# Routing in two parts, and combine's identity products ordered behind the last expert

## The chip, the cores and the metric

The kernel runs on one core of one Trainium2 chip. The number that counts is the device time of one execution in microseconds (us). The core has five engines that run side by side, each through its own instructions strictly in order: TensorE (PE in the profile, with its weight loads as PEld), VectorE (DVE), ScalarE (ACT), GpSimd (POOL) and SyncE (SP), which here only issues loads. An instruction whose operands are not ready holds back everything that stands behind it on its engine.

## The reference

The model is two layers (DEPTH 2) on 512 tokens of width 1024. A layer is a token mixer with three branches and then a mixture of experts. Only the second half matters here:

```python
def grouped_moe(x, router_w, router_b, w1, w3, w2):       # x: 512 tokens x 1024
    logits = (xt @ router_w).astype(jnp.float32) + router_b
    scores = jax.nn.softmax(logits, axis=-1)               # 16 experts in 4 groups of 4
    grp_score = lax.top_k(scores.reshape(T, 4, 4), 2)[0].sum(-1)
    best = jnp.argmax(grp_score, axis=-1)                  # one group for each token
    in_group = (jnp.arange(16) // 4)[None, :] == best[:, None]
    top_w, top_e = lax.top_k(jnp.where(in_group, scores, -1.0), 2)
    gates = top_w / jnp.sum(top_w, axis=-1, keepdims=True)
    ...                                                    # tokens sorted by expert
    hb = jax.nn.silu(xb @ w1[e]) * (xb @ w3[e])
    return hb @ w2[e]                                      # 1024 x 1024 weights each
    ...                                                    # gated rows summed back per token

h = layer_norm(ALPHA * h + y, ln2_g[l], ln2_b[l])
```

So each token goes to the two best experts of its best group, and its output is the gated sum of two expert rows plus the residual, normalised.

## The kernel before

**Arithmetic.** Nearly all products are in 32-bit floating point made of three reduced products: a weight tile `raw` of 128x1024 is split into a rounded part `wh` (a cast on ScalarE, L342) and the rest `wl` (a subtraction on VectorE, L343), activations likewise, and `mm3` (L345 to L350) adds high x high, high x low and low x high. Lines 348, 349 and 350 are thus nearly all of TensorE's work. A split into `wl` that names GpSimd as its engine runs there: this is done for the first four tiles of the first expert of each layer.

**Tokens** come in four blocks of 128 (NT is 4), and everything that depends on a token is laid out as 128 partitions by 4 blocks.

**Routing.** After the mixer, `logits` makes the 128x16 logits of one block at a time: transposes, products with the router weights into the PSUM bank `lg` (a bank of kind "o", of which there is one), and two VectorE instructions (L1057, L1058) that apply the norm to them. `keep_awake` then puts 15 dummy products on TensorE (L1081). `route` (L1083 on) works on all four blocks at once: the row maximum `mx`, the difference `s`, the exponential on ScalarE, some 19 small VectorE instructions that end in the 0/1 matrix `M` (L1118) of each token's two experts, then eight small products that count, for each token, how many earlier tokens chose the same expert (L1122, L1125) and how many chose each expert in all (L1128). They go to a bank `rk`. The rank within the expert is `rke` (L1131); `cn` (L1133) is a copy of the counts.

**Gather products.** `one_hot` (L1244) compares `rke` with an iota and gives a 0/1 matrix `A`, one 128x256 piece per block, for the first two experts. 64 products (L1358: 4 blocks by 8 column chunks k by 2 for the high and low half of the token rows) pick the tokens of those experts into eight banks `gx`; banks of the chunks 0 to 6 are of other kinds, the last chunk's is the bank "o". The token rows of the last block are normalised just before by `settle`, which is told to come behind the exponential and behind the last piece of `A`: two ScalarE instructions (L296), four on VectorE (L299), two casts to the high half on ScalarE (L1071) and two subtractions for the low half on VectorE (L1072). Then the chunks are copied to `hx` and the experts begin. `gates` (L1141 on) makes the gate weights with small VectorE instructions meanwhile.

**Experts and combine.** Fourteen experts have 96 fixed slots each. Their outputs go to DRAM (`yd`), except those of two experts, of which one is the last: they stay on the chip as `ywh` and `ywl` (`last_y`, L1487 and L1488). At the end of the layer `collect` gathers for each block c the two expert rows of each token with indirect DMAs from GpSimd's queue into `yg` (L1467) and adds the two (L1473): the left half of the columns on VectorE, the right half on GpSimd, both issued behind the last weight split. `add_known` (L1447) starts the sum of a block in two PSUM banks `cmb` with what is known, and `combine` adds the sum `yg` by a product with the identity matrix (L1559) and the last expert's rows by two products (L1561). There are eight identity products in a layer, two for each block. The norm of the result follows; in the last layer it is the end of the program.

**What sets the order.** The program is written for a scheduler that puts the instructions of each engine in one fixed order by priority and expected readiness; `issue_after(x)` forbids it to place an instruction ahead of x, without adding a wait. On TensorE this fixed order is what counts below, since a product early in it that waits for another engine stops all the later ones.

## Time and profile before

| | |
|---|---|
| runs, us | 2222.1, 2217.58, 2212.92 (median 2217.58) |
| profiled execution, us | 2214.86 |
| its span, first to last instruction, us | 2213.1 |
| TensorE busy | 2114.7 us, 96% |
| VectorE busy | 1545.0 us, 70% |
| ScalarE busy | 1230.4 us, 56% |
| GpSimd busy | 505.0 us, 23% |
| mean granted TensorE clock | 0.976 |

The span is the time between the first and the last instruction on the core; the 1.8 us around it belong to the execution but show no instruction. A busy share is a mean over stages, so the table says only that TensorE is the engine that most stages wait for: a microsecond that TensorE loses is mostly a microsecond of the time, and one that another engine loses is felt only where TensorE waits for it or at the very end.

### The profile page before, as it was taken

Reading aid. Unit: us, or ns where it says so; the run is one execution under the profiler, and the core shown is the slowest. Engines: PE = TensorE matmul, PEld = TensorE weight load, DVE = VectorE, ACT = ScalarE, POOL = GpSimd, SP = SyncE. Lnnn points to the kernel's source line nnn. Section 1 sums busy time; section 2 is a strip of 40 time slices with the busy share of each in tenths; the row PEclk is TensorE's granted clock in tenths of the full one; section 3 lists DMA queues with packets and bytes.
Section 4 is the critical chain, followed back from the end, with each engine's and each line's share of the span. In section 5 each row is a group of like instructions: output and inputs, shape, how many; then the busy total and the mean of one; then the engine's idle time right before and its main releaser. Section 6 shows DMA issues by size and latency. Waiting matters only on the chain. (4 is left out here: it accounts for less than half of the span.)

```text
span 2213.1 us, 27508 instructions
## 1 busy us (share of the span) xinstructions
PE 2114.7 (96%) x10178; PEld 1557.3 (70%) x10181; DVE 1545.0 (70%) x1986; ACT 1230.4 (56%) x1548; POOL 505.0 (23%) x535
## 2 busy tenths in 40 slices
PE   6999999998999999998899999999899999999987
PEld 5668678876777766665666877888767776666664
DVE  8443533459999899887663535434799998888877
ACT  4333123336888777776544331223488887777763
POOL 5410142122039825000260202411410000000004
PEclk9988999999999999999999999999999999999999
DMA  5121275337999999998731213352499999999973
GB/s 192 54 52 53 65 246 194 103 121 280 385 346 375 375 368 340 376 379 315 260 138 45 76 57 124 105 190 96 148 347 386 388 385 352 380 364 380 365 301 130
DMA packets 192461, 533.16 MB, mean 241 GB/s; under 512 B 18545, under 2 KB 72433, under 8 KB 192306
## 3 DMA queue, kind: packets, MB, share of 16 engines
q1 hardware_dynamic: 173312, 476.69, 58.2%
q0 software_dynamic: 8032, 28.84, 3.9%
q10 hardware_dynamic: 10962, 25.67, 3.4%
q8 instruction: 84, 1.38, 0.3%
q14 instruction: 71, 0.58, 0.1%
HBM read 501.14 MB, written 27.00 MB: 239 GB/s over the span
## 5 line engine op out<-in xcount | busy, mean ns | idle before, releaser
L343 DVE TENSOR_TENSOR wl<-raw,wh 128x1024 fp32r<-128x1024 f32 x850 | 1042.3, 1261 | 345.5 <-ACT wh L342 310.6
L342 ACT CAST wh<-raw 128x1024 fp32r<-128x1024 f32 x872 | 896.0, 1050 | 426.7 <-PE e L350 152.8
L349 PE MATMUL e<-wl,hx 128*96 128x512 f32 x1024 | 408.9, 399 | 9.4 <-DVE wl L343 9.4
L350 PE MATMUL e<-wh,hx 128*96 128x512 f32 x1024 | 408.2, 399 | 0.0
L348 PE MATMUL e<-wh,hx 128*96 128x512 f32 x1024 | 383.4, 397 | 10.0 <-PEq L1496 9.9
L348 PE MATMUL pjf<-hx,wh 128*128 128x512 f32 x608 | 244.7, 403 | 4.8 <-DVE v L215 4.8
L350 PE MATMUL pjf<-hx,wl 128*128 128x512 f32 x608 | 244.2, 402 | 2.5 <-DVE wl L343 2.5
L349 PE MATMUL pjf<-hx,wh 128*128 128x512 f32 x608 | 244.6, 402 | 0.8 <-DVE hx L216 0.7
L349 PEld LDWEIGHTS e<-wl,hx 128*96 128x96 f32 x1024 | 167.0, 163 | 86.0 <-DVE wl L343 20.0
L348 PEld LDWEIGHTS e<-wh,hx 128*96 128x96 f32 x1024 | 166.4, 163 | 78.9 <-issue 11.4
L350 PEld LDWEIGHTS e<-wh,hx 128*96 128x96 f32 x1024 | 166.9, 163 | 66.1 <-issue 0.6
L349 PE MATMUL e<-wl,gh 128*96 128x512 f32 x512 | 204.0, 398 | 5.9 <-DVE wl L343 5.4
L350 PE MATMUL e<-wh,gl 128*96 128x512 f32 x512 | 201.2, 394 | 2.6 <-DVE gl L1267 2.6
L1182 POOL DMA_INDIRECT xr<-xd,idx x28 | 46.3, 1655 | 655.8 <-PE tx L1264 523.2
L348 PE MATMUL e<-wh,gh 128*96 128x512 f32 x512 | 180.2, 394 | 0.0
L348 PEld LDWEIGHTS pjf<-hx,wh 128*128 128x128 f32 x608 | 115.9, 191 | 33.4 <-DVE v L215 6.0
L350 PEld LDWEIGHTS pjf<-hx,wl 128*128 128x128 f32 x608 | 115.7, 190 | 29.5 <-DVE wl L343 3.0
L349 PEld LDWEIGHTS pjf<-hx,wh 128*128 128x128 f32 x608 | 115.7, 190 | 29.2 <-DVE hx L216 1.9
L349 PEld LDWEIGHTS e<-wl,gh 128*96 128x96 f32 x512 | 82.6, 161 | 49.8 <-DVE wl L343 18.1
L348 PEld LDWEIGHTS e<-wh,gh 128*96 128x96 f32 x512 | 82.5, 161 | 35.3
L350 PEld LDWEIGHTS e<-wh,gl 128*96 128x96 f32 x512 | 82.5, 161 | 35.2 <-DVE gl L1267 3.5
L956 POOL TENSOR_TENSOR mg<-mg,gsg 128x512 f32<-128x512 f32 x32 | 42.9, 1345 | 211.6 <-DVE gsg L955 187.3
(500 smaller groups left out, 2823.4 us busy)
## 6 DMA issues: line engine op xcount, KB each, us to landing
raw<-in_moe_w_dram SPq DMA_DIRECT2D x384, 1024.0 KB, 7.7
raw<-in_w_in_dram SPq DMA_DIRECT2D x44, 1024.0 KB, 5.3
yd<-y ACTq DMA_DIRECT2D x28, 384.0 KB, 6.0
raw<-in_w_out_dram SPq DMA_DIRECT2D x8, 1024.0 KB, 5.0
yd<-zr ACTq DMA_DIRECT2D x14, 384.0 KB, 5.2
row<-hd POOLq DMA_DIRECT2D x8, 512.0 KB, 7.1
rawu<-in_w_up_c_dram SPq DMA_DIRECT2D x8, 512.0 KB, 3.4
xd<-row POOLq DMA_DIRECT2D x8, 512.0 KB, 3.6
```

The source lines that it names most:

```text
L342: self.cut = (nc.scalar.copy(hv, v).ins, (eng or nc.vector).tensor_tensor(lv, v, hv.bitcast(F32), OP.subtract).ins)
L343: (eng or nc.vector).tensor_tensor(lv, v, hv.bitcast(F32), OP.subtract).ins)
L348: mm(out, lh, rh, start=start, stop=False)
L349: mm(out, lh, rl, start=False, stop=False)
L350: mm(out, ll, rh, start=False, stop=stop)
L956: nc.gpsimd.tensor_tensor(mg[m], mg[m], sg, OP.add)
L1182: self.fetched = self.nc.gpsimd.indirect_dma_start(out=t, out_offset=None, in_=self.x_dram[:, :], in_offset=at).ins
```

## The change

1. `route` runs its chain of small instructions twice: for the blocks 0 to 2 together, then for block 3. Ranks of the first part depend on the first three blocks alone, so `A` of these blocks can be made before the last block's logits have gone through the chain. The counts are summed once at the end.
2. The rank products no longer have a bank of their own: they go into free columns of the logits' bank `lg`, which is therefore held until the copy `cn` (now L1140) has been made. This bank is the only one of kind "o", which is also the bank of the last gather chunk.
3. In `collect` both halves of the sum are added on VectorE (L1482); GpSimd only gathers.
4. In `combine` all identity products (now L1569) are issued behind `self.near`, the last product of step k = 6 of the last expert's second weight matrix, that is, nearly behind the whole last expert.

The core of the diff, without the lines of the chain that are only indented:

```diff
-        mm(out, ll, rh, start=False, stop=stop)
+        self.product = mm(out, ll, rh, start=False, stop=stop).ins
...
-            lps = self.bank("o", "lg")
+            lps = self.lps = self.bank("o", "lg")
...
+        ps = self.lps[:, 2 * P:3 * P]
...
+        for c0, c1 in ((0, NT - 1), (NT - 1, NT)):
+            nt = c1 - c0
+            col = lambda x, n: x[:, :, None].to_broadcast([P, nt, n])
+            mx, s, gs, gm, gw, M, rke = (x[:, c0:c1] for x in (mx_, s_, gs_, gm_, gw_, M_, rke_))
+            w, sums = [x[:, 4 * c0:4 * c1] for x in w_], sums_[:, 4 * c0:4 * c1]
+            V.tensor_reduce(mx, lg[:, c0:c1], AX.X, OP.max)
+            V.tensor_tensor(s, lg[:, c0:c1], col(mx, NE), OP.subtract)
+            ex = nc.scalar.activation(s, s, AF.Exp)
...
-        ps = self.bank("o", "rk")
-        f = lambda x: x.rearrange("p c e -> p (c e)")
-        nc.tensor.matmul(ps[:, 0:64], self.before_b, f(M), start=True, stop=False, skip_group_check=True)
...
+            own = ps[:, c0 * NE:c1 * NE]
+            nc.tensor.matmul(own, self.before_b, f(M), start=True, stop=False, skip_group_check=True)
+            for c in range(c1 - 1):
+                to = max(c + 1, c0)
+                n = c1 - to
...
+            pr = own.rearrange("p (c e) -> p c e", c=nt)
+            last = V.scalar_tensor_tensor(rke, pr, 1.0, M, OP.add, OP.mult)
         for c in range(NT):
-            nc.tensor.matmul(ps[:, 64:80], self.ones_b, M[:, c], start=c == 0, stop=c == NT - 1, skip_group_check=True)
+            nc.tensor.matmul(ps[:, 64:80], self.ones_b, M_[:, c], start=c == 0, stop=c == NT - 1, skip_group_check=True)
...
+                if k == 6:
+                    self.near = self.product
...
-                for i, eng in enumerate((nc.vector, nc.gpsimd)):
+                for i in range(2):
                     sl = slice(i * 512, (i + 1) * 512)
-                    eng.tensor_tensor(yg[0][:, sl], yg[1][:, sl], yg[0][:, sl], OP.add)
+                    nc.vector.tensor_tensor(yg[0][:, sl], yg[1][:, sl], yg[0][:, sl], OP.add)
...
-                nc.tensor.matmul(self.cmb[c][n], self.ident, self.acc[c][:, ns], start=False, stop=False)
+                with self.tc.issue_after(self.near):
+                    nc.tensor.matmul(self.cmb[c][n], self.ident, self.acc[c][:, ns], start=False, stop=False)
```

How the instructions stand on an engine is fixed when the program is built, so it can be read without a run. First TensorE in the routing of the first layer, before: `rk` are the rank products, `gx` the gather products (only the first rows of these are shown), `cb` a constant.

```order
L1122 MATMUL rk<-M,cb 128x64 [waits DVE_49]
L1125 MATMUL rk<-M,cb 128x48
L1125 MATMUL rk<-M,cb 128x32
L1125 MATMUL rk<-M,cb 128x16
...
L1358 MATMUL gx<-A,hi 128x256 [waits DVE_49]
L1358 MATMUL gx<-A,hi 128x256 x5
```

And the same place after the change, where the rank products write into `lg`:

```order
L1132 MATMUL lg<-M,cb 128x16
L1367 MATMUL gx<-A,hi 128x256 [waits DVE_49]
...
L1367 MATMUL gx<-A,hi 128x256 [waits DVE_49]
L1367 MATMUL gx<-A,hi 128x256 x13
...
L1128 MATMUL lg<-M,cb 128x16 [waits DVE_49]
...
L1138 MATMUL lg<-M,cb 128x16 [waits DVE_49]
...
L1367 MATMUL gx<-A,hi 128x256 [waits Activation_49]
```

The rank products of block 3 (L1128 128x16) and the counts (L1138) now stand behind 42 gather products: those of the chunks 0 to 6 for the blocks 0 to 2. The other 22 follow: two of block 3, the six of the last chunk for the blocks 0 to 2, and 14 of block 3.

VectorE at the same place, before (the chain between `mx` and `M` left out):

```order
L1058 SCALAR_TENSOR_TENSOR lg<-lg,ve,rc 128x16 [waits DVE_49,Pool_49]
L1089 TENSOR_REDUCE mx<-lg 128x4 [waits DVE_49]
L1090 TENSOR_TENSOR s<-lg,mx 128x64 [waits DVE_49]
...
L1118 SCALAR_TENSOR_TENSOR M<-w_3817,gw 128x64 [waits DVE_49]
L1131 SCALAR_TENSOR_TENSOR rke<-rk,M 128x64 [waits DVE_49,PE_49]
L1133 COPY cn<-rk 128x80
L1244 TENSOR_TENSOR A<-cs,rke 128x256 [waits DVE_49]
L1244 TENSOR_TENSOR A<-cs,rke 128x256 x3
L299 TENSOR_TENSOR row_2238<-row_2238,lngb 128x512 [waits Activation_49] x2
```

And after the change; `w_3814` to `w_3816`, `gs`, `gm`, `gw` and `oh` are the small tiles of the chain:

```order
L1103 TENSOR_TENSOR s<-lg,mx 128x48 [waits DVE_49]
L1058 SCALAR_TENSOR_TENSOR lg<-lg,ve,rc 128x16 [waits DVE_49,Pool_49]
...
L1123 SCALAR_TENSOR_TENSOR M<-w_3814,gw 128x48 [waits DVE_49]
L1113 TENSOR_REDUCE gm<-gs 128x1 [waits DVE_49]
L1118 TENSOR_TENSOR w_3814<-s 128x8
...
L1136 SCALAR_TENSOR_TENSOR rke<-lg,M 128x48 [waits PE_49]
...
L1251 TENSOR_TENSOR A<-cs,rke 128x256 x2
...
L1136 SCALAR_TENSOR_TENSOR rke<-lg,M 128x16 [waits DVE_49,PE_49]
L1251 TENSOR_TENSOR A<-cs,rke 128x256 [waits DVE_49]
L299 TENSOR_TENSOR row2_2238<-row2_2238,lngb 128x512 [waits Activation_49] x2
```

The difference `s` of the first three blocks has moved ahead of the last block's L1058, five instructions of block 3's chain stand between the first `M` and the first `rke`, and `settle` of block 3 (L299) stands behind the second `rke`, which waits for TensorE.

Third, TensorE in the second weight matrix (`e` from `gh` and `gl`) of the last expert, first layer, before:

```order
L348 MATMUL e_11561<-wh,gh 96x512 [waits Activation_49]
L349 MATMUL e_11561<-wl,gh 96x512
L1559 MATMUL cmb<-yg,cs 128x512 [waits DMASW6_49,Pool_49]
L1447 MATMUL cmb<-hi,idr 128x512 [waits DVE_49]
L1447 MATMUL cmb<-hi,idr 128x512
L1447 MATMUL cmb<-hx,at 128x512 x2
L350 MATMUL e_11561<-wh,gl 96x512
```

And after:

```order
L348 MATMUL e_11585<-wh,gh 96x512 [waits Activation_49]
L349 MATMUL e_11585<-wl,gh 96x512
L1456 MATMUL cmb<-hi,idr 128x512 [waits DVE_49]
L1456 MATMUL cmb<-hi,idr 128x512
L1456 MATMUL cmb<-hx,at 128x512 x2
L350 MATMUL e_11585<-wh,gl 96x512
...
L1569 MATMUL cmb<-yg,cs 128x512 [waits DMASW2_49,DVE_49]
L1571 MATMUL cmb<-ywh,at 128x512 [waits Activation_49]
```

The identity product that stood among the first products of that matrix has moved behind all of them, and it waits for VectorE and no longer for GpSimd. The second layer has the same pattern, with two identity products at that place.

## Rows read from the trace of the kernel before

**Rows 1.** Head of the page: span and instruction count

```profile
span 2213.1 us, 27508 instructions
```

**Rows 2.** Waits of PE: total us, times, longest us

```profile
PE cmb L1559 <- POOL yg L1473: 7.6, 2, 6.1
PE rk L1122 <- DVE M L1118: 6.5, 2, 4.1
...
PE gx L1358 <- DVE A L1244: 4.8, 2, 2.4
```

**Rows 3.** Timeline of PE, last expert of the first layer: start, us, instruction

```profile
1093.48 0.40 PE L349 MATMUL e<-wl,gh 128*96 128x512 f32 x1
1099.97 2.08 PE L1559 MATMUL cmb<-yg,cs 128*128 128x512 f32 x2 [6.09 <-POOL yg L1473]
...
1103.40 0.40 PE L350 MATMUL e<-wh,gl 128*96 128x512 f32 x1
```

**Rows 4.** Timeline of DVE, the same stretch

```profile
1094.27 1.02 DVE L1267 TENSOR_TENSOR gl<-tx,gh 128x384 fp32r<-128x384 f32 x2
1105.61 1.23 DVE L343 TENSOR_TENSOR wl<-raw,wh 128x1024 fp32r<-128x1024 f32 x1 [10.32 <-issue]
...
1113.48 2.48 DVE L1473 TENSOR_TENSOR yg<-yg 128x512 f32<-128x512 f32 x4
...
1117.82 0.73 DVE L1488 SCALAR_TENSOR_TENSOR ywl<-e,gate,ywh 96x512 fp32r<-96x512 f32 x1
```

**Rows 5.** Timeline of POOL, the same stretch

```profile
1106.69 5.77 POOL L1473 TENSOR_TENSOR yg<-yg 128x512 f32<-128x512 f32 x3 [1.90 <-DMA yg<-yd,pos]
1116.04 4.70 POOL L343 TENSOR_TENSOR wl<-raw,wh 128x1024 fp32r<-128x1024 f32 x2 [3.57 <-ACT wh L342]
```

**Rows 6.** Timeline of PE, last expert of the second layer

```profile
2179.84 0.40 PE L350 MATMUL e<-wh,gl 128*96 128x512 f32 x1
```

**Rows 7.** Timeline of DVE, from there to the end

```profile
2176.01 1.01 DVE L1267 TENSOR_TENSOR gl<-tx,gh 128x384 fp32r<-128x384 f32 x2
...
2205.61 4.05 DVE L316 SCALAR_TENSOR_TENSOR yg<-yg,ve,lngb 128x512 f32<-128x512 f32 x6
```

**Rows 8.** Timeline of PE, routing of the first layer

```profile
502.89 0.19 PE L1122 MATMUL rk<-M,cb 128*128 128x64 bf16 x1 [2.42 <-DVE M L1118]
...
505.63 9.43 PE L1358 MATMUL gx<-A,hi 128*128 128x256 f32 x64 [2.39 <-DVE A L1244]
515.16 0.48 PE L348 MATMUL e<-wh,hx 128*96 128x512 f32 x1
```

**Rows 9.** Timeline of DVE, routing of the first layer

```profile
495.69 2.19 DVE L1058 SCALAR_TENSOR_TENSOR lg<-lg,ve,rc 128x16 f32<-128x16 f32 x1
497.92 0.22 DVE L1089 TENSOR_REDUCE mx<-lg 128x4 f32<-128x64 f32 x1
498.17 2.07 DVE L1090 TENSOR_TENSOR s<-lg,mx 128x64 f32<-128x64 f32 x1
...
503.28 0.23 DVE L1131 SCALAR_TENSOR_TENSOR rke<-rk,M 128x64 f32<-128x64 f32 x1 [0.44 <-PE rk L1128]
...
503.56 5.20 DVE L1244 TENSOR_TENSOR A<-cs,rke 128x256 fp32r<-128x256 f32 x4
508.69 2.48 DVE L299 TENSOR_TENSOR row<-row,lngb 128x512 f32<-128x512 f32 x4
...
511.30 1.28 DVE L1072 TENSOR_TENSOR hi<-row,hi 128x512 fp32r<-128x512 f32 x2
```

**Rows 10.** Timeline of POOL, routing of the first layer

```profile
495.50 4.65 POOL L343 TENSOR_TENSOR wl<-raw,wh 128x1024 fp32r<-128x1024 f32 x2
502.95 4.86 POOL L343 TENSOR_TENSOR wl<-raw,wh 128x1024 fp32r<-128x1024 f32 x2 [2.79 <-ACT wh L342]
```

**Rows 11.** PE by stretches: stretch, us, busy us (instructions), granted clock, DMA

```profile
507.00:509.00 2.00, 2.00 (x11) 0.50 0.04 14
...
511.00:515.00 4.00, 4.00 (x34) 1.00 0.98 276
```

More of the change, by code (lines that the diff above doesn't have):

```diff
@@ L1086, in route @@
         t = lambda nm, sh, dt=F32: pool.tile([P] + sh, dt, tag=nm, name=nm, bufs=1)
[L1087 to L1094 removed]
+        mx_, s_ = t("mx", [NT]), t("s", [NT, NE])
@@ L1095, in route @@
+        w_ = [t(f"w{i}", [16, 4]) for i in range(3)]
+        sums_ = t("oh", [128])[:, 0:96].rearrange("p (g n) -> p g n", g=16)
+        gs_, gm_, gw_ = t("gs", [NT, 4]), t("gm", [NT]), t("gw", [NT, 4])
+        M_, rke_ = t("M", [NT, NE], BF16), t("rke", [NT, NE])
         pair = (([0, 2], [1, 3]), ([0, 1], [2, 3]), ([0, 1], [3, 2]))
+        ps = self.lps[:, 2 * P:3 * P]
         def at(x, i):
             return x[:, :, i[0]:(i[1] + (1 if i[1] > i[0] else -1)) if i[1] or i[1] > i[0] else None:i[1] - i[0]]
-        for i, (lo, hi) in enumerate(pair):
-            V.tensor_tensor(sums[:, :, 2 * i:2 * i + 2], at(s4, lo), at(s4, hi), OP.add)
@@ L1122, in route @@
-        nc.tensor.matmul(ps[:, 0:64], self.before_b, f(M), start=True, stop=False, skip_group_check=True)
-        for c in range(NT - 1):
-            n = NT - 1 - c
-            nc.tensor.matmul(ps[:, (c + 1) * NE:64].rearrange("p (c e) -> p c e", c=n), self.ones_b,
-                             M[:, c:c + 1].to_broadcast([P, n, NE]), start=False, stop=c == NT - 2, skip_group_check=True)
+        for c0, c1 in ((0, NT - 1), (NT - 1, NT)):
[6 more added lines that the diff above has]
+            ex = nc.scalar.activation(s, s, AF.Exp)
+            s4 = s.rearrange("p c (g e) -> p (c g) e", g=4)
+            for i, (lo, hi) in enumerate(pair):
+                V.tensor_tensor(sums[:, :, 2 * i:2 * i + 2], at(s4, lo), at(s4, hi), OP.add)
+            r4 = self.misc[:, None, 32:36].to_broadcast([P, nt, 4])
+            V.tensor_reduce(gs.rearrange("p c g -> p (c g)"), sums, AX.X, OP.max)
+            for i, (lo, hi) in enumerate(pair):
+                V.tensor_tensor(at(w[i], lo), at(s4, lo), at(s4, hi), OP.is_ge)
+                if i == 0:
+                    V.tensor_reduce(gm, gs, AX.X, OP.max)
+                if i == 1:
+                    V.tensor_tensor(gw, gs, col(gm, 4), OP.is_equal)
+                if i == 2:
+                    V.tensor_tensor(gw, gw, r4, OP.mult)
+                V.tensor_tensor(at(w[i], hi), at(s4, hi), at(s4, lo), OP.is_gt)
+            V.tensor_tensor(w[0], w[0], w[1], OP.add)
+            V.tensor_reduce(gm, gw, AX.X, OP.max)
+            V.tensor_tensor(w[0], w[0], w[2], OP.add)
+            V.tensor_tensor(gw, gw, col(gm, 4), OP.is_equal)
+            V.scalar_tensor_tensor(M.rearrange("p c (g e) -> p (c g) e", g=4), w[0], 2.0,
+                                   gw.rearrange("p c g -> p (c g)")[:, :, None].to_broadcast([P, 4 * nt, 4]),
+                                   OP.is_ge, OP.mult)
+            f = lambda x: x.rearrange("p c e -> p (c e)")
+            own = ps[:, c0 * NE:c1 * NE]
[3 more added lines that the diff above has]
+                n = c1 - to
+                nc.tensor.matmul(ps[:, to * NE:c1 * NE].rearrange("p (c e) -> p c e", c=n), self.ones_b,
+                                 M_[:, c:c + 1].to_broadcast([P, n, NE]), start=False, stop=c == c1 - 2,
+                                 skip_group_check=True)
+            pr = own.rearrange("p (c e) -> p c e", c=nt)
+            last = V.scalar_tensor_tensor(rke, pr, 1.0, M, OP.add, OP.mult)
```

32 lines of the change are left out of this document (1 added, 31 removed).

## The prediction

> **What bounds the kernel now.** I read the head of the page first, for the span against which the sum is made [rows 1]. Then the view of TensorE's waits, since TensorE is busy nearly throughout: the change aims at three of its entries [rows 2]. Combine's identity product waits for GpSimd's additions, 7.6 us in two waits, one of them 6.1; the rank products wait for `M`, 6.5 us in two; the gather products wait for `A`, 4.8 us in two. That is 18.9 us, once per layer each, and as much as removing them could bring if nothing took their place. Then the timelines of the engines around these waits, to see what would be late next.
>
> **Combine, first layer.** TensorE stands at the identity product from 1093.7, goes on at 1099.97 and reaches the next weight product only at 1103.40 [rows 3]. That product needs `gl`, which VectorE has ready at 1094.27 + 1.02 = 1095.3 [rows 4]. The four products of `add_known` stay in front of it, and they are done by then or some 0.5 us later. So the expert's second matrix can go on at about 1095.3, 1103.40 − 1095.3 = 8.1 us earlier. The identity product itself (the row counts its two passes, 2.08 us at a clock that has fallen, so some 1.0 us at the full one) is not saved but moved behind the matrix: 7.1 us.
>
> Some of it is given back at once. The additions come after the last weight split on VectorE in both kernels. Before, VectorE had four of them, 2.48 us, and GpSimd four; now VectorE has eight. I cost the four new ones at 0.62 each, 2.5 us; about half lies in the time in which VectorE waits for the last expert's end, since the rows show it idle before the last splits (10.32 us idle before the one at 1105.61) and it is no longer tied to GpSimd's three slow additions there (5.77 us [rows 5]). The next layer's first splits run on GpSimd from 1116.04, behind the combine's work before; when the combine moves forward they meet the additions and `ywl` more than before. The full gain is 7.1, and next to nothing is gained if all four additions and two held instructions of 2.3 us (4.70 / 2 in the row) fall on the path: 7.1 − 2.5 − 4.7 = −0.1. I take 5.5, nearer to the full gain, since VectorE's last `ywl` at 1117.82 then only has to come forward to 1112.3, and about 5 us of its wait before 1113.48 have gone. Ends kept: 0 and 8.
>
> **Combine, second layer.** The same step is smaller: the wait is 7.6 − 6.1 = 1.5 us [rows 2]. The weight product at 2179.84 [rows 6] can start after `gl` at 2177.0 [rows 7], 2.8 us earlier. Two identity products, 2.0 us, go from there to the end of the matrix, where TensorE waits for the last expert's rows in any case. What follows is VectorE's normalisation to the end of the program (the last six instructions alone take 4.05 us to 2209.7), and the four new additions, 2.5 us, stand on that engine, ahead of it. I take −2.0, nearer to the full 2.8 since VectorE waits for the last matrix before its additions can matter; the ends are −2.8 and, with both costs on the path, +1.7.
>
> **Routing.** Here the instructions that move are few and short, but they move into a bad place. Before, the sequence from the last logits is: L1058 at 495.69, `mx`, `s` at 498.17, ranks at 502.89, `rke` at 503.28, `A` from 503.56, the gather products from 505.63 to 515.1, and the first expert at 515.16 [rows 8, 9]. Three steps take much longer than their size: L1058 (2.19 us for 16 columns), `s` (2.07 us for 64) and the four `A` (5.20 us together). They begin while a split runs on GpSimd (two from 495.50, two from 502.95 [rows 10]) and end when it does. `mx`, which has a single input from SBUF, takes 0.22 us in the same stretch, and `rke`, which reads PSUM, 0.23. One instruction of VectorE with two SBUF inputs gets through for every split of GpSimd.
>
> [...]
>
> Now the new order. `s` of the first three blocks takes the hold of the first split, L1058 of block 3 that of the second; `mx` and `s` of block 3 and the whole chain come after 500.2. `s` of block 3 ends at about 500.7. From `s` to the rank products it was 502.89 − 500.24 = 2.65 us for the exponential and 19 instructions, so about 0.13 each; the first `M` has 22 instructions before it from there (some of block 3's are mixed in), so the first ranks come at about 503.5 instead of 502.89. The exponential of block 3 goes out 0.5 us later than before, so GpSimd's next two splits (502.95 before) run from about 503.4 to 508.2. Between the first `M` and the first `rke` there are now five instructions of block 3's chain, four with two SBUF inputs. The first is held to 505.8, the second to 508.2. The first `A` follows with three more of them and `rke`: it is done at about 509.0 to 509.5, against 505.6.
>
> Then 42 gather products run. [...] With 20 at 0.18 and 22 at 0.118 the 42 take 6.2 us, to about 515.4. Only then do block 3's ranks get their turn on TensorE, since they stand behind. From there: ranks to `rke` 0.4 (502.89 to 503.28), `rke` and `A` 0.7, then `settle` of block 3, which on VectorE lasted from 508.69 to 511.30 + 1.28 = 512.58, 3.9 us. So the low half of block 3 is ready at 515.4 + 0.4 + 0.7 + 3.9 = 520.4. In the meantime TensorE can do only eight of the other 22 products; up to 14 are left, 1.6 us at the full clock and 2.5 at the half. The first expert starts at 522.0 to 522.9 instead of 515.16: I take +7.0 in each layer, +14 in both, as the second layer's rows repeat the first's.
>
> Why did it not cost this before? `settle` of block 3 lay beside the gather products of the blocks 0 to 2; that cover is gone, since it now stands behind `rke` and `A` of the second part, and these stand behind 42 of the products that had covered it. Bounds: if the holds do not reach the first part, its `A` comes at about 504.6, and the same sum ends at 522.4 − 4.6 = 517.8, +2.6 a layer, 5.3 in all; if the clock stays low longer, +9 a layer, 18 in all. I take the upper part, since holds have shown in every place where these two engines meet in these rows. The gates' small instructions (some ten of 0.2 us) move behind the `hx` copies, into the time of the first expert, whose first splits GpSimd makes; this is cover enough, so zero, or +0.5 a layer without it. The bank `lg` held until `cn` only delays six products, which are counted above.
>
> **Sum.** −5.5 − 2.0 + 14.0 = +6.5. On the profiled execution (2214.86 us, 1.8 us above its span and 2.7 below the median of the runs shown, 2217.58, so a fair sample) that is 2221.4 us.
>
> **Rivals.** First, the holds miss the first part: for it speaks that the first `M` is only some tenths of a microsecond away from GpSimd's third split; against it, five instructions must still pass after `M`. Then 5.3 − 7.5 = −2.2, or 2212.7 us. Second, faster: the products of the first part run early and take the clock up before block 3's arrive, and combine gives all it can. With `A` at 504.6 instead of 505.6, 1 us is won in each layer and nothing is lost behind it: −2.0 − 8.0 − 2.8 = −12.8, 2202 us; against it is the fixed order on TensorE, which puts block 3's ranks behind 42 products. Third, slower: VectorE becomes late in combine. Its place is the stretch between the last split and the last `ywl`, where it has 2.5 us more work per layer and meets GpSimd's first splits of the next layer; its price is the gain of the first layer, 5.5, and half of the second's, 1.0. It decides when the last `ywl` of the first layer comes no earlier than 1117.82 and then the sum is +14.0 − 1.0 = +13.0, 2227.9 us; with the longer low clock, 2232. Fourth, the change does nothing that shows: the two sides cancel fully, 2215 us; it is inside the first two forecasts' range and adds no sign of its own.
>
> **How the numbers follow.** A difference below 0.5%, 11 us, cannot be told from none here. My forecast has 0.50, the first rival 0.22, the fourth 0.05, the faster one 0.08, the slower one 0.15. The first three lie within 0.5%, 0.77 together. The range from 2208 to 2231 holds the forecast with its bounds (2215 to 2226 by itself), the first rival and most of the slower one; it leaves out the faster one.
>
> **What would show it.** In the profile after: TensorE's 6.1 us wait at the identity product is gone and the last expert's second matrix runs through; the first gather product comes after 508 in the first layer; TensorE waits for ScalarE or VectorE (`hi` and `lo` of block 3) between the 42nd gather product and the last; the first expert starts some 7 us later after the last logits than before. The forecast is wrong if the first `A` is done before 506, or if block 3's `settle` runs beside the first gather products, or if the last `ywl` of the first layer is not earlier.

## The result, and the profile after

The changed kernel takes 2227.61 us (median of 14 runs, 2219.04 to 2234.35), the kernel before 2214.58 us beside it (14 runs, 2206.48 to 2228.91). The ratio is 1.0053, interval 1.0032 to 1.0074, so by the ratio about 11.7 us more (7.1 to 16.4): slower, by a size that lies just at the prediction's bound of 0.5%, with the interval on both sides of it. The forecast was 2221.4 us, in a range of 2208 to 2231.

The profiled execution took 2221.57 us, only 6.7 more than that of before. That it meets the forecast's sum is chance. The mixers, whose code the change doesn't touch, happened to take 5.4 us less in this execution (see the last section). The stages are therefore compared one by one, each from one instruction of TensorE or VectorE to another. "Routing" runs from the last logits (VectorE's last L1057) to the first expert's first product; "experts" from there to the first product of the last expert's second matrix; "combine" from there to the next layer's first weight product (layer 1) or to the span's end (layer 2). "Rest" is all other time, whose code is the same in every kernel below, but for two splits of the next layer that e4 and e9 to e12 take off GpSimd. All are us of one profiled execution.

| kernel | routing 1 | experts 1 | combine 1 | routing 2 | experts 2 | combine 2 | six stages | rest |
|---|---|---|---|---|---|---|---|---|
| before | 19.8 | 578.1 | 39.6 | 20.2 | 571.8 | 38.1 | 1267.6 | 945.5 |
| after | 25.1 | 580.3 | 40.6 | 24.3 | 573.3 | 36.1 | 1279.7 | 940.1 |
| e1_route_only | 24.2 | 580.6 | 40.4 | 24.9 | 572.3 | 38.2 | 1280.5 | 954.1 |
| e2_combine_both | 19.8 | 578.2 | 33.3 | 20.2 | 571.7 | 36.1 | 1259.4 | 942.9 |
| e3_order_only | 19.5 | 578.4 | 44.2 | 19.7 | 572.2 | 36.0 | 1270.0 | 954.6 |
| e4_combine_nohold | 19.8 | 578.6 | 33.4 | 19.5 | 571.4 | 36.1 | 1258.8 | 960.1 |
| e5_gates_early | 25.0 | 577.8 | 40.2 | 24.4 | 570.5 | 36.1 | 1274.0 | 946.1 |
| e6_ranks_early | 22.1 | 577.8 | 40.0 | 22.7 | 571.1 | 36.2 | 1269.9 | 955.2 |
| e7_two_splits_after | 21.7 | 580.5 | 33.1 | 23.6 | 573.8 | 36.2 | 1268.9 | 945.0 |
| e8_two_splits_before | 19.0 | 582.0 | 40.2 | 17.1 | 572.6 | 41.9 | 1272.8 | 939.7 |
| e9_split_all | 17.8 | 582.3 | 34.0 | 16.8 | 576.7 | 36.1 | 1263.7 | 953.2 |
| e10_nosplit_all | 19.0 | 584.4 | 35.4 | 17.8 | 572.5 | 36.2 | 1265.2 | 944.6 |
| e11_split_late | 22.0 | 579.7 | 34.1 | 20.4 | 573.8 | 36.1 | 1266.1 | 954.2 |
| e12_nosplit_late | 19.7 | 580.0 | 33.7 | 19.2 | 570.3 | 36.1 | 1259.1 | 944.8 |

After against before, the six stages give +9.4 in routing, +3.7 in the experts, +1.0 in combine 1 and −2.0 in combine 2: +12.1, which agrees with the 11.7 measured over the runs. "Rest" scatters over 20 us with the same instructions, so one execution's whole time says little here.

TensorE's waits in the kernel after (us in total, times, longest) answer to [rows 2]:

```profile
PE cmb L1571 <- DVE ywl L1497: 6.4, 1, 6.4
PE lg L1128 <- DVE M L1123: 6.0, 2, 3.6
PE gx L1367 <- DVE A L1251: 5.9, 2, 3.0
PE gx L1367 <- ACT hi L1071: 5.3, 2, 2.7
...
PE e L350 <- DVE hx L1274: 4.2, 2, 2.1
```

The wait for GpSimd's additions is gone. The waits for `M` and for `A`, at which the change aimed, are still there with 11.9 us in place of 11.3. Three large entries are new: `ywl` in combine, `hi` in the routing, `hx` among the experts.

**Routing.** TensorE in the first layer after (start, us, instruction), against [rows 8]. The last L1057 starts here at 488.55, and at 495.36 in the kernel before, so times are compared from there.

```profile
495.61 0.18 PE L1128 MATMUL lg<-M,cb 128*128 128x48 bf16 x1 [3.64 <-DVE M L1123]
...
498.79 7.30 PE L1367 MATMUL gx<-A,hi 128*128 128x256 f32 x42 [2.97 <-DVE A L1251]
505.93 0.18 PE L1128 MATMUL lg<-M,cb 128*128 128x16 bf16 x1
...
509.37 4.39 PE L1367 MATMUL gx<-A,hi 128*128 128x256 f32 x22 [2.67 <-ACT hi L1071]
513.60 0.40 PE L348 MATMUL e<-wh,hx 128*96 128x512 f32 x1
```

The first gather product starts 498.79 − 488.55 = 10.24 us after the last logits: not a tenth earlier than before (10.27). The 42 products then run 7.3 us, the ranks of block 3 come only behind them, and TensorE waits 2.67 us for block 3's `hi`. VectorE and GpSimd show why nothing was won in front, against [rows 9, 10]:

```profile
488.69 0.20 DVE L1103 TENSOR_TENSOR s<-lg,mx 128x48 f32<-128x48 f32 x1
488.88 2.26 DVE L1058 SCALAR_TENSOR_TENSOR lg<-lg,ve,rc 128x16 f32<-128x16 f32 x1
...
495.86 0.21 DVE L1136 SCALAR_TENSOR_TENSOR rke<-lg,M 128x48 f32<-128x48 f32 x1
...
496.13 5.45 DVE L1251 TENSOR_TENSOR A<-cs,rke 128x256 fp32r<-128x256 f32 x3
...
506.43 0.43 DVE L1251 TENSOR_TENSOR A<-cs,rke 128x256 fp32r<-128x256 f32 x1
```

```profile
496.11 4.86 POOL L343 TENSOR_TENSOR wl<-raw,wh 128x1024 fp32r<-128x1024 f32 x2 [2.71 <-ACT wh L342]
```

A VectorE instruction is called held below where it lasts until a GpSimd split beside it has ended. `M` and `rke` of the first part are through by 496.07. GpSimd's third split starts at 496.11, and the three `A`, which start at 496.13, are held: they last 5.45 us beside the two splits; the one `A` at 506.43, with GpSimd idle, lasts 0.43. The clock under the 42 products (stretch, us, busy us and count, granted clock, DMA share and GB/s; [rows 11]):

```profile
500.00:502.00 2.00, 2.00 (x12) 0.50 0.00 0
502.00:504.00 2.00, 2.00 (x13) 0.66 0.89 270
504.00:506.00 2.00, 2.00 (x21) 1.00 0.65 262
```

After TensorE's wait of 2.97 us they run at a granted clock of 0.50 until past 502, as the 64 of before did at first (0.50 from 507 to 509, [rows 11]).

**Combine, first layer.** TensorE, against [rows 3]:

```profile
1094.17 0.40 PE L349 MATMUL e<-wl,gh 128*96 128x512 f32 x1
...
1096.59 0.40 PE L350 MATMUL e<-wh,gl 128*96 128x512 f32 x1
...
1107.21 1.02 PE L1569 MATMUL cmb<-yg,cs 128*128 128x512 f32 x2
...
1115.77 0.79 PE L1571 MATMUL cmb<-ywl,at 96*128 96x512 f32 x1 [6.44 <-DVE ywl L1497]
```

The weight product L350 follows 2.4 us behind L349, where it was 9.9 us before: the removed wait is removed. But TensorE stands at 1109.3, for 6.44 us, for `ywl`, and from 1115 to 1121 its granted clock is 0.50, where it was 1.00 from 1115 to 1121 before. VectorE, then GpSimd, against [rows 4, 5]:

```profile
1105.05 1.29 DVE L1482 TENSOR_TENSOR yg<-yg 128x512 f32<-128x512 f32 x2 [0.87 <-DMA yg<-yd,pos]
1108.26 6.79 DVE L1482 TENSOR_TENSOR yg<-yg 128x512 f32<-128x512 f32 x4 [1.91 <-DMA yg<-yd,pos]
1114.98 0.73 DVE L1497 SCALAR_TENSOR_TENSOR ywl<-e,gate,ywh 96x512 fp32r<-96x512 f32 x1
```

```profile
1086.38 5.71 POOL L1476 DMA_INDIRECT yg<-yd,pos  x1 [136.17 <-DVE wl L343]
...
1100.01 0.95 POOL L1476 DMA_INDIRECT yg<-yd,pos  x1 [0.30 <-issue]
1108.42 5.48 POOL L343 TENSOR_TENSOR wl<-raw,wh 128x1024 fp32r<-128x1024 f32 x2 [7.47 <-ACT wh L342]
```

Two additions take 1.29 us, the next four 6.79 us: they begin 0.16 us ahead of GpSimd's two splits for the next layer and end 1.15 us after them. `ywl` stands behind them on VectorE. They are this late because the last gathers are: the first gather on GpSimd took 5.71 us, the later ones 0.94 to 1.05.

**Combine, second layer.** Here no next layer follows. From the first product of the second matrix to the end it is 36.1 us, against 38.1.

**Experts.** The third expert's L350 waits 2.10 us for `hx` in each layer, and from 582 to 586 us, behind the first of these waits, the granted clock is 0.59 (0.50 until 585, then 0.86). VectorE is late, since small instructions now stand between the weight splits. They belong to `places` (L1236 is one of its 37), which works out where each token's two rows lie in `yd`. It ends 68.4 us behind the first expert's first product, and ended at 60.8 before; the twelve instructions of `gates` end at 13.0 and ended at 2.4. TensorE, then VectorE:

```profile
580.45 0.71 PE L350 MATMUL e<-wh,hx 128*96 128x512 f32 x2 [2.10 <-DVE hx L1274]
```

```profile
578.55 1.22 DVE L343 TENSOR_TENSOR wl<-raw,wh 128x1024 fp32r<-128x1024 f32 x1
579.69 0.16 DVE L1236 TENSOR_TENSOR pf<-pf,xs 128x8 f32<-128x8 f32 x1
...
579.84 0.55 DVE L1274 TENSOR_TENSOR hx<-tx,hx 128x384 fp32r<-128x384 f32 x1
```

### The profile page after: what moved, and what is told of

Same layout as the page of the kernel before. It is cut to its first block, busy times and chain, and to the rows that moved or that the text cites. A ratio compares the mean times of both kernels' runs of the same rounds, so it can differ in the third digit from the quotient of the medians.

```text
span 2219.8 us, 27562 instructions
## 1 busy us (share of the span) xinstructions
PE 2114.6 (95%) x10186; PEld 1560.8 (70%) x10187; DVE 1551.3 (70%) x2036; ACT 1231.1 (55%) x1550; POOL 490.8 (22%) x527
## 5 line engine op out<-in xcount | busy, mean ns | idle before, releaser
L349 PE MATMUL e<-wl,hx 128*96 128x512 f32 x1024 | 408.9, 399 | 9.4 <-DVE wl L343 9.4
L350 PE MATMUL e<-wh,hx 128*96 128x512 f32 x1024 | 408.1, 399 | 4.2 <-DVE hx L1274 4.2
L350 PE MATMUL pjf<-hx,wl 128*128 128x512 f32 x608 | 243.4, 400 | 2.5 <-DVE wl L343 2.5
L349 PE MATMUL pjf<-hx,wh 128*128 128x512 f32 x608 | 244.1, 401 | 0.5 <-DVE hx L216 0.4
L349 PEld LDWEIGHTS e<-wl,hx 128*96 128x96 f32 x1024 | 167.1, 163 | 85.5 <-DVE wl L343 19.2
L348 PEld LDWEIGHTS e<-wh,hx 128*96 128x96 f32 x1024 | 166.9, 163 | 80.0 <-issue 12.6
L350 PEld LDWEIGHTS e<-wh,hx 128*96 128x96 f32 x1024 | 166.5, 163 | 70.9 <-DVE hx L1274 5.1
L349 PE MATMUL e<-wl,gh 128*96 128x512 f32 x512 | 204.2, 399 | 4.8 <-DVE wl L343 4.0
L350 PE MATMUL e<-wh,gl 128*96 128x512 f32 x512 | 201.1, 393 | 0.1
L350 PEld LDWEIGHTS pjf<-hx,wl 128*128 128x128 f32 x608 | 115.4, 190 | 29.2 <-DVE wl L343 2.9
L349 PEld LDWEIGHTS pjf<-hx,wh 128*128 128x128 f32 x608 | 115.3, 190 | 28.7 <-DVE hx L216 1.5
L349 PEld LDWEIGHTS e<-wl,gh 128*96 128x96 f32 x512 | 82.6, 161 | 48.3 <-DVE wl L343 16.0
L350 PEld LDWEIGHTS e<-wh,gl 128*96 128x96 f32 x512 | 82.5, 161 | 32.8 <-DVE gl L1274 1.1
```

What stands on the lines that cost most here:

```text
L348: mm(out, lh, rh, start=start, stop=False)
L349: mm(out, lh, rl, start=False, stop=False)
L350: self.product = mm(out, ll, rh, start=False, stop=stop).ins
```

## The experiments

**e1: the routing alone.** The kernel before with parts 1 and 2 of the change; collect and combine as before.

```diff
-            lps = self.bank("o", "lg")
+            lps = self.lps = self.bank("o", "lg")
...
+        for c0, c1 in ((0, NT - 1), (NT - 1, NT)):
```

> The routing in two parts alone, combine as before. Stages are read from the trace: routing from VectorE's L1057 of the last block to the first expert's first product (19.8 us in the first layer and 20.2 in the second before, 25.1 and 24.3 after the whole change); experts from there to the first product of the last expert's second matrix (578.1 and 571.8 before, 580.3 and 573.3 after). Theory: all of the loss is in these stages, +5 and +4 in routing, +1.5 to +2.2 in the experts of each layer, so +13 us, a ratio of 1.005 to 1.007, with combine's stages at 39.6 and 38.1 as before. Rival: combine's new order costs, and routing only part: +5 us or less here.

2227.68 us against 2218.3, ratio 1.0055 (1.0026 to 1.0084), +12.2 us; by stages +12.9. The routing, with what it does to the experts, is the whole of the loss that can be measured.

**e2: combine alone.** Parts 3 and 4 of the change, routing as before.

```diff
+                if k == 6:
+                    self.near = self.product
...
-                    eng.tensor_tensor(yg[0][:, sl], yg[1][:, sl], yg[0][:, sl], OP.add)
+                    nc.vector.tensor_tensor(yg[0][:, sl], yg[1][:, sl], yg[0][:, sl], OP.add)
...
+                with self.tc.issue_after(self.near):
+                    nc.tensor.matmul(self.cmb[c][n], self.ident, self.acc[c][:, ns], start=False, stop=False)
```

> Combine's order and the additions on VectorE, routing as before. Combine of the first layer is read from the first product of the last expert's second matrix to the next layer's first product (39.6 us before, 40.6 after the whole change), of the second layer from that product to the end of the span (38.1 before, 36.1 after). Theory: +1 and -2, so -1 us in all, a ratio of 0.998 to 1.001. Rival (the new order costs, and routing only part of the loss): +5 us or more, 1.002 and above.

By the stages −8.2 us, with combine 1 at 33.3 in place of 40.6 in after, by the same code: better than the theory had it, and against the rival. The runs say 2219.96 us, 1.0016 (0.9992 to 1.0041). GpSimd and VectorE in this profile:

```profile
1077.04 1.20 POOL L1469 DMA_INDIRECT yg<-yd,pos  x1 [136.08 <-DVE wl L343]
...
1099.10 5.54 POOL L343 TENSOR_TENSOR wl<-raw,wh 128x1024 fp32r<-128x1024 f32 x2 [9.97 <-ACT wh L342]
```

```profile
1097.15 2.50 DVE L1475 TENSOR_TENSOR yg<-yg 128x512 f32<-128x512 f32 x4 [1.09 <-DMA yg<-yd,pos]
...
1100.23 2.19 DVE L1475 TENSOR_TENSOR yg<-yg 128x512 f32<-128x512 f32 x1
```

The first gather took 1.20 us, the four additions had all begun (2.50 us) before GpSimd's splits did, and only the next two additions were held (2.19 and 1.58 us). In this code the gathers decide a race between the additions and GpSimd's splits (won where all four begin before the splits; in after only the first of them does), and the same instructions come out 7 us apart. The profile says what a won race is worth; it can't say how often it is won, and the runs show no gain.

**e3: the order alone**, additions on both engines as before.

```diff
-                for i in range(2):
+                for i, eng in enumerate((nc.vector, nc.gpsimd)):
...
-                    nc.vector.tensor_tensor(yg[0][:, sl], yg[1][:, sl], yg[0][:, sl], OP.add)
+                    eng.tensor_tensor(yg[0][:, sl], yg[1][:, sl], yg[0][:, sl], OP.add)
```

> Combine's order alone: the identity products behind the last expert, but the additions half on VectorE and half on GpSimd as before; routing as before. Theory (in the changed kernel VectorE's additions are held by GpSimd's first splits of the next layer, two instructions): with GpSimd's additions in its queue ahead of these splits, VectorE has four additions fewer and is held less, so combine of the first layer takes 35 to 38 us (39.6 before, 40.6 after), that of the second 36 to 37. Rival (the identity products at the end are simply in TensorE's way, whatever adds): 40 us or more in the first layer.

2223.74 us, 1.0016 (0.9993 to 1.0039); combine 1 took 44.2, more than before's 39.6. That is the rival's number, but not for its reason, as e2 has the same order and takes 33.3. TensorE, then GpSimd, then VectorE:

```profile
1111.52 2.08 PE L1562 MATMUL cmb<-yg,cs 128*128 128x512 f32 x2 [3.75 <-DVE yg L1475]
...
1119.50 0.79 PE L1564 MATMUL cmb<-ywl,at 96*128 96x512 f32 x1 [5.47 <-DVE ywl L1490]
```

```profile
1110.82 4.67 POOL L1475 TENSOR_TENSOR yg<-yg 128x512 f32<-128x512 f32 x3 [2.36 <-DMA yg<-yd,pos]
1115.45 5.54 POOL L343 TENSOR_TENSOR wl<-raw,wh 128x1024 fp32r<-128x1024 f32 x2
```

```profile
1113.50 5.28 DVE L1475 TENSOR_TENSOR yg<-yg 128x512 f32<-128x512 f32 x3 [2.04 <-DMA yg<-yd,pos]
```

With GpSimd's slow additions and its splits back to back, VectorE's own additions are held through both and `ywl` stands behind them. So in the first layer the new order needs the additions on VectorE; in the second it does by itself what both edits do (36.0). The additions on VectorE without the new order were not run.

**e4: combine without GpSimd's next-layer splits.** e2, with the first weight splits of the next layer's mixer on VectorE.

```diff
-LEND = ((...), ("11", "00", "00", "00", "01", "01", "01", "01", "00"))
+LEND = ((...), ("00", "00", "00", "00", "01", "01", "01", "01", "00"))
```

> As e2, with the next layer's first two weight splits on VectorE instead of GpSimd, so that nothing on GpSimd meets the additions. Theory (holding): the additions of the first layer take about 0.65 us each (four in 6.79 us after the change), the wait of 6.4 us at the last expert's products shrinks to 1 to 3 us, and combine of the first layer takes 34 to 37 us. Rival (eight additions or the gathers' landing are too much for VectorE by themselves): 39 us or more and the wait above 4 us.

2214.56 us, 0.9983 (0.9957 to 1.0008); six stages −8.8. The additions began 14.0 us behind the second matrix's start, in after 14.3, in e2 12.6; and yet, on VectorE:

```profile
1107.89 2.50 DVE L1475 TENSOR_TENSOR yg<-yg 128x512 f32<-128x512 f32 x4 [1.71 <-DMA yg<-yd,pos]
```

Without GpSimd's splits late additions cost 2.50 us and not 6.79, the wait for `ywl` is 1.8 us and not 6.4, and combine 1 takes 33.4. The hold is the cause in after. The four later kernels that have no GpSimd splits there (e9 to e12) agree, with 33.7 to 35.4.

e5 to e8 were executed once each (2221.89, 2226.95, 2215.75 and 2214.3 us, before beside them 2226.53), so only their stages are read.

**e5: the gates' instructions back.** After, with the gates' small instructions placed behind `M`.

```diff
+            with tc.issue_after(r["m"]):
+                self.gates(r, self.hi)
...
-                        self.gates(r, self.hi)
```

> The changed kernel, with the small instructions of the gates ordered right behind block 3's M, where VectorE waits for TensorE in any case, instead of among the first experts' splits. Theory (these instructions, and what was pushed on by them, make VectorE late for the third expert's rows): routing stays at 25.1 and 24.3 us (within 0.8), the experts fall back from 580.3 and 573.3 to 578.0 to 578.7 and 571.6 to 572.3, and the waits of 2.1 us for hx go. Rival (the experts take longer because they start later, or through the rows' fetch on GpSimd): 580 and 573 stay.

Experts 577.8 and 570.5, 2.5 and 2.8 less than after and even under before; no wait for `hx` at the third expert's L350 is left, and `places` ends at 60.8 us again. Routing (25.0, 24.4) and combine are those of after. So the loss in the experts goes where `places` is on time again. That the gates push it back is not settled by this: in e6, where the gates end at 11.2 us, `places` ends at 61.1 and the experts take 577.8 and 571.1.

**e6: block 3's ranks behind 14 gather products**, not 42: the products of the blocks 1 and 2 are put behind the ranks.

```diff
+            self.ranked = nc.tensor.matmul(ps[:, 64:80], self.ones_b, M_[:, c], ...).ins
...
+                            with tc.issue_after(self.ranked) if c else ExitStack():
+                                nc.tensor.matmul(ps[k][:, s * 256:(s + 1) * 256], rows[c][:, k * P:(k + 1) * P],
```

> The changed kernel, with the gather products of the blocks 1 and 2 ordered behind block 3's rank products, so that these stand behind 14 gather products and no longer behind 42. Theory (the order on TensorE is the loss): settle of block 3 runs beside the 28 others, the wait of 2.7 us for hi goes, and routing takes 20 to 21.5 us instead of 25.1 and 24.3. Rival (the low clock after the wait, or the splits on GpSimd, are the loss): 23.5 us or more.

Routing 22.1 and 22.7, between the theory and the rival: 3.0 and 1.6 us of the loss go, with the wait for `hi`. Some 2.4 us stay. The products start no later than in before (10.23 us after the last logits), but they pause for the ranks and stay at a granted clock of 0.50 for longer:

```profile
507.67 3.35 PE L1369 MATMUL gx<-A,hi 128*128 128x256 f32 x14 [2.96 <-DVE A L1252]
...
511.80 7.88 PE L1369 MATMUL gx<-A,hi 128*128 128x256 f32 x50
```

```profile
511.00:513.00 2.00, 1.59 (x14) 0.50 0.95 276
513.00:515.00 2.00, 2.00 (x12) 0.50 0.59 238
515.00:517.00 2.00, 2.00 (x17) 0.86 0.54 94
```

The granted clock is 0.50 until 515 and 0.86 on the mean of the next 2 us, after two waits and the short pause for the ranks.

**e7 and e8: GpSimd's third and fourth split taken off it**, in after (e7) and in before (e8). VectorE makes them later.

```diff
-            for u in range(2):
+            for u in range(1):
```

> The changed kernel, with only the first two of the first expert's four early weight splits made on GpSimd; the other two are made on VectorE like all later ones. Theory (GpSimd's third and fourth split hold A): the three A of the first part take 1.2 to 1.5 us instead of 5.45, the first gather product comes 8.0 to 8.8 us after the last block's L1057 instead of 10.2, and routing takes 22.5 to 23.5 us (the 42 products still stand ahead of block 3's ranks). Rival (A is slow by itself, or the start hangs on something else): 10 us and 24 or more.

> The kernel before, with only the first two early splits on GpSimd. Theory (holding): the four A take 1.6 to 1.9 us instead of 5.20, the first gather product comes 8.4 to 8.9 us after the last L1057 instead of 10.3, and routing takes 17.5 to 18.7 us instead of 19.8; the two added splits on VectorE lengthen the first expert by 0 to 2.5 us. Rival: routing within 0.5 us of 19.8.

VectorE and TensorE of e7:

```profile
495.08 1.09 DVE L1251 TENSOR_TENSOR A<-cs,rke 128x256 fp32r<-128x256 f32 x3
```

```profile
495.56 5.30 PE L1367 MATMUL gx<-A,hi 128*128 128x256 f32 x42 [0.78 <-DVE A L1251]
```

Three `A` take 1.09 us, not 5.45, and the gather products start 2.2 us earlier than in after. In before (e8) four `A` take 1.42 us, not 5.20, and its routing falls to 19.0 and 17.1:

```profile
496.96 1.42 DVE L1244 TENSOR_TENSOR A<-cs,rke 128x256 fp32r<-128x256 f32 x4
```

So what TensorE had waited for at `A` was GpSimd's splits, with or without the two parts. Where both kernels are free of them, the two parts are still slower, 21.7 and 23.6 against 19.0 and 17.1. The experts of e8, where VectorE makes the two splits, take 3.9 and 0.8 more. Its combine, whose code is before's, took 41.9 in the second layer, as TensorE waited 3.78 us there for GpSimd's addition and 1.49 in before: this wait differs between executions.

**e9 and e10: all that helped, with two parts and with one.** e9 is after with e4's, e5's, e6's and e7's edits, and VectorE's two splits kept behind block 3's `settle`; e10 is e4 with the same treatment of the splits, on before's routing.

```diff
+                        after.enter_context(tc.issue_after(self.chosen))
+                        after.enter_context(tc.issue_after(self.settled))
```

> All that the runs so far point to, with the routing in two parts: block 3's ranks behind 14 gather products (as e6), the gates' instructions right behind its M (as e5), the first expert's third and fourth early split on VectorE, ordered behind settle (as e7), combine's order with all additions on VectorE and the next layer's first splits off GpSimd (as e4). Theory: the first gather product 8.1 us after the last L1057, routing 16.2 to 18 us in each layer (19.8 and 20.2 before), experts 578 to 580.5 and 572 to 574, combine 33.3 and 36.1: -10 to -14 us, a ratio of 0.9935 to 0.9965. Rival (what is won in routing comes back in the experts through VectorE's two added splits): 0.997 or more.

> The same with the routing in one part as before the change: the first expert's third and fourth early split on VectorE behind settle, combine as e4. It tells what the two parts are worth once nothing holds them. Theory (with the hold gone the four A take 1.4 us and the parts win 1 to 2 us more in each layer, no more): routing 17 to 19 us, experts 579 to 582 and 572 to 574, combine 33.3 and 36.1, a ratio of 0.995 to 0.998, 2 to 4 us behind e9. Rival (the parts are worth nothing or cost): level with e9 or faster.

e9: 2211.01 us, 0.9974 (0.9949 to 0.9999), of nine kernels with an interval the one whose interval lies below 1, and by 0.0001 only; the ratio is the rival's, not the theory's. e10: 2212.3 us, 0.9989 (0.9967 to 1.0011). e9 has the shortest routings of all, 17.8 and 16.8, 1.2 and 1.0 less than e10. That is what the two parts, with e5's and e6's edits, gave where no hold met them, in one profile of each. The experts of e9 take 4.2 and 4.9 more than before, those of e10 6.3 and 0.7; combine gives e9 −5.6 and −2.0. The six stages of the two are 1.5 us apart and the runs don't tell them apart, so a gain by the two parts is not shown.

**e11 and e12: those two splits back on GpSimd, but later**, behind block 3's `hi`; with two parts (e11), with one (e12).

```diff
+                for kk in range(2):
+                    with tc.issue_after(self.settled):
+                        ready.append(self.split_half(tiles[1][:, kk:kk + 1, :], (1, 1024), nc.gpsimd))
```

> As e9, but the first expert's third and fourth early split go back to GpSimd, behind settle's casts on ScalarE, so that they begin when A is done. Theory (e9's loss in the experts, +4.2 and +4.9 us, is VectorE's two added splits): routing 16.5 to 18.5 us in each layer, experts 577.5 to 579.5 and 570.5 to 573, combine 33.3 to 34 and 36.1: -10 to -15 us against before, a ratio of 0.993 to 0.9955. Rival (the late splits on GpSimd hold the gates' instructions and with them the hx copies): routing 19 us or more, ratio 0.997 or more.

> As e10 (routing in one part), with the same two splits on GpSimd behind settle's casts. Theory: routing 17.5 to 19.5 us (the gates' four two-input instructions stand ahead of the hx copies and may be held once or twice by 2.3 us), experts 578 to 580 and 571.5 to 573, combine 33.3 to 34 and 36.1: -8 to -12 us, a ratio of 0.9945 to 0.9965, so that the two parts in e11 are worth 1 to 4 us. Rival (the parts are worth nothing): e11 and this one within 1 us in routing and experts together.

e11: 2218.6 us against 2220.28, 0.9992 (0.9965 to 1.0019); e12: 2216.03 us, 0.9982 (0.9958 to 1.0006). In e11 the splits met the gates' instructions instead, as its rival had it. GpSimd, then VectorE:

```profile
505.47 4.71 POOL L343 TENSOR_TENSOR wl<-raw,wh 128x1024 fp32r<-128x1024 f32 x2 [0.75 <-ACT wh L342]
```

```profile
505.32 0.26 DVE L1156 CAST R<-G 128x64 bf16<-128x64 f32 x1
505.61 2.34 DVE L1157 TENSOR_TENSOR v<-G,R 128x64 f32<-128x64 f32 x1
507.99 2.29 DVE L1158 CAST R<-v 128x64 bf16<-128x64 f32 x1
...
510.69 1.41 DVE L1263 CAST hx<-gx 128x256 fp32r<-128x256 f32 x4
```

The copies `hx` of the first expert stand behind these and come at 510.69. TensorE's waits have an entry for them (total, times, longest), and routing is back at 22.0 and 20.4:

```profile
PE e L348 <- DVE hx L1263: 6.7, 2, 3.8
```

e12, with the chain in one piece, keeps 19.7 and 19.2 and has six stages of 1259.1 (−8.5). Its runs lie 4.0 us lower than before's, with an interval that reaches from 9.3 lower to 1.3 higher, short of the ratio expected. Here the two parts cost 7.0 us by the stages (e11 against e12), where a gain of 1 to 4 was expected.

## Where the prediction was right, and which of its steps were wrong

The measured time lies in the stated range and above before, as forecast. The sum behind it is right in part only, and that the total lies so near is partly luck: two terms were too low and one was too high.

**Routing (+14.0 forecast, +9.4 measured).** The mechanism held in its second half: block 3's ranks behind 42 products, its `settle` uncovered, TensorE waiting for `hi`. The failed step is where the holds fall. The forecast gave the first split's hold to `s` of the first three blocks, with block 3's exponential 0.5 us later for it, and let the next two holds hit the five instructions between the first `M` and the first `rke`, so that the first gather product would start at 509.2, 13.8 us after the last logits. But `s` took 0.20 us, and block 3's exponential came 4.92 us after the last logits, the exponential of before 4.91. The chain was about 1 us quicker than forecast, `rke` slipped through just before the third split, and the splits hit the three `A`: 10.24 us. By its own sign this step was wrong, since the first `A` was done 10.2 us after the last logits and 506 stands for 10.6. That took 3.6 us off the first layer and 3.5 off the second. The 42 products gave 0.9 back (7.14 us to the ranks, not 6.2, for the clock). No run shows the 6.2 us: the forecast put 20 products at 0.18 us and 22 at 0.118, the paces at 0.50 and at 1.00 in [rows 11], while in after the granted clock was 0.50 until 502 and 0.66 from there to 504. From there to the first expert it took 7.67 us, not 6.75: `hi` came 3.44 us behind the ranks, where the forecast waited 5.0 for the low half, but then all 22 products were left, 4.2 us, and not 14, since the first of the 22 is one of block 3 and stops the others. Sum in the first layer 7.0 − 3.6 + 0.9 + 0.9 = 5.2, measured 5.25; in the second 4.1. The first rival, in which the holds miss the first part, was half right: they missed `M` and `rke` and caught `A`. e7 shows that `A` is held by the splits; e6 that the order on TensorE costs 3.0 and 1.6 us of the rest.

The hold itself shows at `A`: three took 1.09 us without GpSimd's splits beside them (e7) and 5.45 with them (after). What in the hardware makes it, no run shows. Which instruction was caught hung on 0.04 us between the end of `rke` and the start of a split. It was no accident of one execution, though: in both layers of all four profiles with the two parts and the four early splits (after, e1, e5, e6) `rke` starts 0.23 to 0.25 us ahead of the third split and the first `A` 0.02 to 0.04 behind it.

**The gates' instructions (0 to +0.5 a layer forecast, +2.2 and +1.5 measured).** The step "GpSimd makes the first splits, cover enough" failed. The loss is not in the first expert: `places` comes late and stands among VectorE's splits for the third expert, where TensorE then waits 2.10 us for `hx`. e5, with the gates early, gives all of it back, and so does e6, with the gates still behind; so what pushes `places` back stays open.

**Combine, first layer (−5.5 forecast, +1.0 measured).** The wait and its removal were as forecast. The failed step is what is given back: 2.5 us for the additions at their free price, half of it hidden, where four additions beside GpSimd's splits took 6.79. Counted from the second matrix's first product, the last `ywl` came 2.3 us earlier (22.3 for 24.6), not 5.5, and what follows it took 3.2 us longer, at a granted clock of 0.50 from 1115 to 1121, behind the 6.44 us wait; the forecast had no term for that clock. This is the third rival's place and mechanism, though not its condition, since `ywl` did come earlier. The forecast's own end near zero (7.1 − 2.5 − 4.7) had both costs together; the rival was given 0.15. It isn't certain either: e2 and e7 ran the same code with the race won (33.3 and 33.1), after, e5 and e6 with it lost (40.6, 40.2, 40.0). e4 and e9 to e12, without GpSimd's splits there, show that the hold is the cause.

**Combine, second layer (−2.0 forecast, −2.0 measured).** All kernels with the new order and all additions on VectorE show 36.1 or 36.2, and e3, with the order alone, 36.0: the four new additions, whose cost the forecast weighed, cost nothing here. The size of what is removed varies, as before's code shows 38.1, 38.2 and 41.9 (before, e1, e8).

**Sum.** Forecast −5.5 − 2.0 + 14.0 = +6.5; by the stages +1.0 − 2.0 + 9.4 + 3.7 = +12.1. Routing was put 4.6 too high, combine 1 6.5 too low, the experts 3.7 too low or nearly. So the time came near the third rival's total of +13.0, with a smaller routing and a cost that no rival had.

**Open.** How often the race in combine is lost: it was lost in three of the five profiles with this combine and GpSimd's splits (after, e5, e6, not e2, e7), which is too few to tell. e2's runs lie 3.5 us above before (−1.8 to 9), while its stages are 8.2 below; a race that is often lost would explain it, and so might the scatter of the rest, and no run tells the two apart.

## What to carry to other kernels

Cutting a chain in two so that its first half starts early gained nothing where another engine held the first half's last step (10.24 us to the first gather product, 10.27 before), and it cost what the second half had as cover; look at what runs beside that step before cutting. The time of a small VectorE instruction did not follow its size where GpSimd split weights beside it: `s` took 0.20 us or 2.07, and other held ones 2.19 (L1058) to 2.34 (L1157). Which instruction was caught was decided by hundredths of a microsecond (0.04 at `A`), so give both ends and a chance to each. Where the same unchanged code scatters by more than the change is worth, compare stages and not whole executions.

## What the runs showed of the hardware that was not expected

**The clock of unchanged code.** In the stretch from 73 to 99 us after the second layer's first weight product, the mixer's products ran at a granted clock of 1.00 in before and of 0.50 in e4, with the same code and TensorE busy for 19.36 and 20.00 of 20 us (columns as for the clock above; before, then e4):

```profile
1212.00:1232.00 20.00, 19.36 (x109) 1.00 0.15 28
```

```profile
1200.00:1220.00 20.00, 20.00 (x78) 0.50 0.00 1
```

Summed over the mixers (busy time times what the granted clock lacks to 1.00), before loses 22 us in layer 1 and 5 in layer 2, e4 22 and 22, after 14 and 7. In the 14 profiles a layer loses 5 to 7, 12 to 14 or 21 to 23 us, and nothing between. "Rest" rises with the sum of both layers, from 939.7 at 20 us lost (e8) to 960.1 at 45 (e4), so this is the greater part of its scatter. In the runs the clock goes the same way: of those of before beside e11 the shortest, 2207.17 us, has a mean granted clock of 0.980, the longest, 2233.41, one of 0.966. What sets the length of these stretches stays open.

**A held instruction with one SBUF input.** L1158 in e11, a cast of 64 columns from f32 to bf16, took 2.29 us in both layers, in the first beside a GpSimd split, and L1156, of the same shape, took 0.26, begun 0.15 us ahead of the splits. So two inputs, by which the forecast told the instructions that are held, are not needed for a hold. What decides which can be held, no run shows.

**A gather's issue.** The first indirect gather of `collect` in the first layer took 1.20 us in e2 and e7 and 5.71 or 5.72 in the other twelve profiles, beside four VectorE splits, which stand close together there. In the twelve its issue ends 0.84 or 0.85 us behind the fourth split (in after the split at 1091.25, the issue at 1092.09); in e2 and e7 three gathers (1.20, 1.95 and 1.95 us) are issued in the same 5.7 us. That VectorE's splits hold the issue is the author's estimate from these times; no run took the splits away. With the additions on VectorE the last gather ends some 2.5 us later where only one passes, and this decided the race in combine. Why three passed in two profiles, no run shows.
